# Writing down the order of a GatedDeltaNet + Conformer layer: waits per step in the heads stage, and three engines held to the order in which the kernel is written

## The chip, the cores and the metric

The kernel runs on one core of one Trainium2 chip. The metric is the device time of one execution in microseconds, the median of several runs. Below, PE is TensorE, DVE is VectorE, ACT is ScalarE, POOL is GpSimd, SP is SyncE (it issues the weight loads). Lines L... of this part are those of the kernel before.

## What is computed

One layer on 512 tokens of width 2048, float32, with about 260 MB of weights read once. Cut to what matters here:

```python
h = rmsnorm(x, g_pre)
qkv, z_a, b_raw, a_raw, glu_in, z_b, gate_logits = split(h @ w_in)

# branch A: gated delta rule, 16 heads of 128, chunks of 64 tokens
qkv = silu(causal_depthwise_conv(qkv, w_conv_qkv))      # 4 taps
beta, g_log = sigmoid(b_raw), -exp(a_log) * softplus(a_raw + dt_bias)
A = (k beta) k^T * decay * strict_lower;  T = inverse(I + A)   # per chunk
for each of 8 chunks:                                    # state S, 128x128 per head
    v_new = T(v beta) - T(k beta exp(gc)) S
    o     = (q exp(gc)) S + (q k^T * decay) v_new
    S     = S exp(g_last) + k_end^T v_new
y_a = (rmsnorm(o) * silu(z_a)) @ w_br_a

# branch B: GLU, causal depthwise conv of 31 taps, layernorm, silu, gate
y_b = (silu(layernorm(conv31(glu(glu_in)))) * silu(z_b)) @ w_br_b

mixed = (gate_a * y_a + gate_b * y_b) @ w_out
x = x + rmsnorm(mixed);  x = x + rmsnorm(sigmoid(x @ w_ple_gate) * (p @ w_ple_proj))
```

## The kernel before

The large products run as **tiles** of 48 matmuls 128x512 (`gemm_cm`): each output tile `g` of 128 channels by 512 tokens sums 16 blocks of the inner dimension, and each block takes three matmuls, since every float32 operand is split in a high and a low part (weight high by `rh`, weight high by `rl`, weight low by `rh`; L178, L180, L182). The weights come in pieces of four blocks (12 matmuls). `prep` loads two pieces at a time into `raw` (SP), ACT rounds them to the high part (L125, "CAST w<-raw") and DVE subtracts to get the low part (L126, called the low split below). `next_piece` calls `prep` when fewer than three pieces are ready, so a piece is split two to four pieces ahead of its use; the ring `w` holds four.

All other work is written as Python generators that are spawned with a period and advanced by `tick()` after every large matmul. So a step's place in the program is counted in ticks, one tick being one large matmul. The jobs of the heads stage are, for each of eight groups of two heads: tiles k, q, v of the first head, k, q, v of the second, then `group(g)` is spawned (period HP = 4), then the two z tiles. While the group's generator advances, the tiles z, z of its own and k, q, v, k, q, v of the next group run: 8 x 48 = 384 ticks.

At the end of each k, q or v tile, `conv4` runs the 4-tap convolution out of the tile's PSUM bank: one ACT operation (L404, `cv<-g`), three DVE operations on the same `cv` one after the other (L406), and then a SiLU on ACT (L415 `kc`, L424 `kq`, L431 `vc`).

`group(g)` does, in this order:
- the *prelude*: per head, PE transposes `pk`, `pq`, `pv` into two PSUM buffers of pool `wps`, sums of squares on ACT, scaled copies `ke` and `vh` on DVE, then `pg` (PE) and the masked `W` (DVE);
- the *inversion*: four ACT copies into `Ud` (L575), a DVE transpose `UT`, 31 steps of a DVE product and a DVE reduction (`prod`, `VT`; L591, L592), a transpose `Vd`, four ACT copies into `VP` and DVE transposes `Tc`, then the small PE products `py`, `pz`, `pd`;
- the *scan* (`head_scan`, both heads side by side): eight chunks of PE `psA` (needs the state `S`), DVE `Xz` and ACT `O` from it, PE `psB` (needs `Xz`), ACT `vz` from it, PE `psS` (needs `vz`), DVE `S`. In chunk 0 there is no `psA`, and `Xz` is an ACT copy of `vh` (L455).

After the heads stage come branch A's output tiles interleaved with the gates and the 31-tap convolution (`dwconv`, DVE), then the layer norm and the z tiles of branch B, branch B's output tiles, the output product (Strassen-like, L1016 to L1066) and the last gate.

The order on each engine is not the written one. A scheduler in the library places the instructions by its own model of when each is ready; the written position only ranks them. Its orders are quoted in the section on the change. In the trace each engine's instructions stand in the listed order.

Of the kernel before, what the change touches and what calls it, by code (L numbers as in the profile page):

```python
# [15 lines left out]
P = 128  # L16
T = 512
# [65 lines left out]
def _body(ctx, tc, A, out):  # L83
# [20 lines left out]

    def cc(col, n=P):
        return cst[:, col:col + n]
# [6 lines left out]
    prepped = deque()  # L113

    def prep():
        if not prep_src:
            return
        src = prep_src.popleft()
        raw = rawp.tile([P, 1024], F32, tag="raw", name="raw", bufs=3)
        nc.sync.dma_start(raw, src)  # L120
        for q in range(2):
            rq = raw[:, q * T:(q + 1) * T]
            w = ring.tile([P, 1024], F32R, tag="w", name="w")
            hi, lo = w[:, 0:T], w[:, T:]
            nc.scalar.copy(hi, rq)  # L125
            nc.vector.tensor_tensor(lo, rq, hi.bitcast(F32), ALU.subtract)  # L126
            prepped.append((hi, lo))
# [37 lines left out]
    def gemm_cm(src, rhs, evac):  # L165
# [3 lines left out]
        def job():  # L169
            ps = gps.tile([P, T], F32, tag="g", name="g")  # L170
            for qt in range(4):
                hi, lo = next_piece()
                for kk in range(4):
# [4 lines left out]
                    mm(ps, wh, rh, start=(k == 0), stop=False)  # L178
                    tick()
                    mm(ps, wh, rl, start=False, stop=False)  # L180
                    tick()
                    mm(ps, wl, rh, start=False, stop=(k == NK - 1))  # L182
# [82 lines left out]


# [26 lines left out]
    def beta_decay(ps):  # L293
        sb = hd.tile([32, T], F32, tag="cv", name="ba_cm")
        nc.scalar.copy(sb, ps[0:32, :])
        yield
        pt = wps.tile([P, T], F32, tag="w", name="ba_t")
        for tt in range(NTT):
            nc.tensor.transpose(pt[:, tt * 32:(tt + 1) * 32], sb[:, tt * P:(tt + 1) * P], cst[0:32, C_ID:C_ID + 32])
        yield  # L300
        ptv = pt[:, 0:128].rearrange("p (t x) -> p t x", x=32)
        nc.scalar.activation(beta, ptv[:, :, 0:NH], AF.Sigmoid)
# [5 lines left out]
        def tl(nm):  # L308
# [3 lines left out]
        nc.vector.tensor_tensor(av.rearrange("p (t h) -> p t h", h=NH), ptv[:, :, NH:2 * NH],  # L312
                                vv(V_DT, NH).unsqueeze(1).broadcast_to([P, NTT, NH]), ALU.add)
        na = tl("na")
        nc.vector.scalar_tensor_tensor(na, av, -1.0, av, ALU.mult, ALU.min)
        e = tl("e")
        nc.scalar.activation(e, na, AF.Exp)
        ea = hp1.tile([P, NH], F32, name="ea")
        nc.scalar.activation(ea, vv(V_ALOG, NH), AF.Exp)
        yield  # L320
        den = tl("den")
        nc.vector.tensor_scalar(den, e, 2.0, None, ALU.add)
        rden = tl("rden")
        nc.vector.reciprocal(rden, den)
        z = tl("z")
        nc.vector.tensor_tensor(z, e, rden, ALU.mult)
        z2 = tl("z2")
        nc.vector.tensor_tensor(z2, z, z, ALU.mult)
        s = tl("s")
        nc.vector.tensor_scalar(s, z2, 1.0 / 17.0, 1.0 / 15.0, ALU.mult, ALU.add)  # L330
        for m in range(13, 0, -2):
            nc.vector.tensor_tensor(s, s, z2, ALU.mult)
            nc.vector.tensor_scalar(s, s, 1.0 / m, None, ALU.add)
            yield
        nc.vector.tensor_tensor(s, s, z, ALU.mult)
        r = tl("r")
        nc.vector.tensor_scalar(r, av, 0.0, None, ALU.max)
        sp = tl("sp")
        nc.vector.scalar_tensor_tensor(sp, s, 2.0, r, ALU.mult, ALU.add)
        g = hp1.tile(TH, F32, name="g_log")  # L340
        nc.vector.scalar_tensor_tensor(g, sp.rearrange("p (t h) -> p t h", h=NH), -1.0,
                                       ea.unsqueeze(1).broadcast_to([P, NTT, NH]), ALU.mult, ALU.mult)
# [3 lines left out]
        mm(pc[:, 0:n], cc(C_CUM), gf, start=True, stop=True)  # L346
        mm(pc[:, n:2 * n], cc(C_BLK), gf, start=True, stop=True)
        mm(pc[:, 2 * n:3 * n], cc(C_HALF0), gf, start=True, stop=True)
        mm(pc[:, 3 * n:4 * n], cc(C_HALF1), gf, start=True, stop=True)
# [3 lines left out]
        nc.vector.tensor_copy(gcf, pc[:, 0:n])  # L353
        dl = tl("dl")
        nc.vector.tensor_tensor(dl, pc[:, n:2 * n], gcf, ALU.subtract)
        nc.vector.tensor_scalar(dl, dl, 0.0, None, ALU.min)
        nc.scalar.activation(ek.rearrange("p t h -> p (t h)"), dl, AF.Exp)
        nc.scalar.activation(eS.rearrange("p a t h -> p (a t h)"), pc[:, 2 * n:4 * n], AF.Exp)
        eg = tl("eg")
        nc.scalar.activation(eg, gcf, AF.Exp)  # L360
        nc.vector.tensor_scalar(neg_eg.rearrange("p t h -> p (t h)"), eg, -1.0, None, ALU.mult)
        yield
        pw = wps.tile([P, T], F32, tag="w", name="sw_ps")
        mm(pw[:, 0:n], cc(C_SWAP), eg, start=True, stop=True)
        nc.vector.tensor_copy(eg_sw.rearrange("p t h -> p (t h)"), pw[:, 0:n])
        blk = hp1.tile([P, P], F32R, name="blk")
        nc.vector.tensor_copy(blk, cc(C_BLK))
        gh = hp1.tile(TH, F32R, name="gh")
        nc.vector.tensor_copy(gh, g)
        gl = hp1.tile(TH, F32R, name="gl")  # L370
        nc.vector.tensor_tensor(gl, g, gh.bitcast(F32), ALU.subtract)
        tri = cst[:, C_TRI:C_TRI + 64].unsqueeze(1).unsqueeze(1).broadcast_to([P, 2, NTT, 64])
        for gi in range(NH // 2):
            tg = []
            for eng, src, tag in ((nc.vector, gh, "ke"), (nc.gpsimd, gl, "vh")):
# [7 lines left out]
            mm(pr, blk, tg[0], start=True, stop=False)  # L383
            mm(pr, blk, tg[1], start=False, stop=True)
# [3 lines left out]
            nc.vector.tensor_tensor(ed, pr.rearrange("p (h t i) -> p h t i", h=2, i=64),  # L388
                                    gcv.unsqueeze(3).broadcast_to([P, 2, NTT, 64]), ALU.subtract)
            edf = ed.rearrange("p h t i -> p (h t i)")  # L390
            nc.vector.tensor_scalar(edf, edf, 0.0, None, ALU.min)
            nc.scalar.activation(edf, edf, AF.Exp)
            nc.vector.tensor_tensor(ed.rearrange("p h t i -> p (h t) i"), ed.rearrange("p h t i -> p (h t) i"),
                                    cst[:, C_TRI:C_TRI + 64].unsqueeze(1).broadcast_to([P, 8, 64]), ALU.mult)
# [6 lines left out]
    def conv4(ps, ct):  # L401
        y = hd.tile([P, T], F32, tag="cv", name="cv")
        w0 = V_CONV + ct * 4
        nc.scalar.activation(y, ps, AF.Copy, scale=vv(w0 + 3))  # L404
        for s in range(1, 4):
            nc.vector.scalar_tensor_tensor(y[:, s:], ps[:, 0:T - s], vv(w0 + 3 - s), y[:, s:], ALU.mult, ALU.add)  # L406
# [4 lines left out]
    def evac_k(h):  # L411
        def f(ps):
            y = conv4(ps, 16 + h)
            kc = hd.tile([P, T], F32, tag="kc", name="kc", bufs=2)
            nc.scalar.activation(kc, y, AF.Silu)  # L415
# [5 lines left out]
    def evac_q(h):  # L421
        def f(ps):
            y = conv4(ps, h)
            nc.scalar.activation(hstate[h]["kq"][:, :, 1:3, :], y.rearrange("p (t x i) -> p t x i", x=2, i=64), AF.Silu)  # L424
        return f

    def evac_v(h):
        def f(ps):
            y = conv4(ps, 32 + h)
            vc = hd.tile([P, T], F32, tag="vc", name="vc", bufs=2)  # L430
            nc.scalar.activation(vc, y, AF.Silu)  # L431
# [3 lines left out]
    def evac_z(h):  # L435
        def f(ps):
            z = hd.tile([P, T], F32, tag="za", name="za", bufs=3)
            nc.scalar.activation(z, ps, AF.Silu)
# [3 lines left out]
    def head_scan(g, hh, G):  # L442
# [6 lines left out]
        for c in range(8):  # L449
# [4 lines left out]
            if c == 0:  # L454
                nc.scalar.copy(X[0:64, :], vh[0:64, 0, :])  # L455
            else:
                pa = sps.tile([P, P], F32, tag="s", name="psA")
                mm(pa, kq[:, tt, 2 * par:2 * par + 2, :].rearrange("p x i -> p (x i)"), S, start=True, stop=True)
                yield
                nc.vector.scalar_tensor_tensor(X[a:a + 64, :], pa[a:a + 64, :], neg_eg[a:a + 64, tt, h:h + 1],  # L460
                                               vh[a:a + 64, tt, :], ALU.mult, ALU.add)
                nc.scalar.activation(O[b:b + 64, tt, :], pa[b:b + 64, :], AF.Copy, scale=eg_sw[b:b + 64, tt, h:h + 1])
            pb = sps.tile([P, P], F32, tag="s", name="psB")
            mm(pb, VP[:, x, :, :].rearrange("p x i -> p (x i)"), X, start=True, stop=True)  # L464
            yield
            if c < 7:
                nc.scalar.activation(vt[a:a + 64, :], pb[a:a + 64, :], AF.Copy, scale=c_all[a:a + 64, x:x + 1])
                pS = sps.tile([P, P], F32, tag="s", name="psS")
                mm(pS, ke[:, tt, :], vt, start=True, stop=True)  # L469
                S2 = hd.tile([P, P], F32, tag="S", name="S", bufs=4)  # L470
                if c == 0:
                    nc.vector.tensor_copy(S2, pS)
# [870 lines left out]
```

## Time and profile before

| | |
|---|---|
| median of 3 runs | 2540.99 us (2539.71 to 2543.15) |
| profiled execution, its own time | 2539.74 us |
| its span, first to last instruction | 2537.1 us |
| PE busy | 2495.0 us, 98% of the span, 12202 matmuls |
| DVE busy | 1652.4 us, 65% |
| ACT busy | 1056.8 us, 42% |
| heads stage with the delta rule | about 128 to 1006 us, one group each 111.5 us |

A row of a window gives, for each engine, the busy time in that window and the number of instructions, then the granted TensorE clock as a share of full speed, the DMA share and GB/s. A row of a timeline gives start and duration in us, the engine and its line, the operation, what it writes and reads, how many were merged, and in brackets the idle time of the engine before it and what ended that.

### The profile page before, as it was taken

What the parts mean: (1) busy time and instruction counts of PE and PEld (TensorE: products, weight loads), DVE (VectorE), ACT (ScalarE), POOL (GpSimd) and SP (SyncE); (2) the same over time, 40 slices, a digit from 0 to 9 for tenths busy, and PEclk for the clock granted to TensorE, in tenths of its full rate; (3) what the DMA queues carried; (4) which work ended last, traced back from release to release, by engine and by line L of the source; (5) the groups of instructions that cost most, each with busy time, mean ns of one, the idle gap of its engine ahead of it and who ended that gap; (6) DMA issues with size and microseconds to landing.
All of it is one profiled execution on the core that took longest, in us unless ns stands there. A gap on an engine that the chain in (4) does not pass through costs nothing.

```text
span 2537.1 us, 32634 instructions
## 1 busy us (share of the span) xinstructions
PE 2495.0 (98%) x12202; PEld 2035.7 (80%) x12202; DVE 1652.4 (65%) x3092; ACT 1056.8 (42%) x2083; POOL 140.6 (6%) x151
## 2 busy tenths in 40 slices
PE   8999999999999999999999999999999999999998
PEld 7878787777878777888888888887888888787887
DVE  6765767666676765977786868947433334777644
ACT  6655455455555455322222222225422222544532
POOL 0100000000000000000000000002000000000000
PEclk9999999999999999999999999999999999999999
DMA  6322222222222222333333332442322332677552
GB/s 257 122 87 71 84 72 83 79 75 88 71 84 71 84 67 75 104 105 102 105 97 107 104 107 98 135 135 92 100 99 93 100 99 92 184 214 224 191 174 75
DMA packets 85406, 279.45 MB, mean 110 GB/s; under 512 B 9472, under 2 KB 9728, under 8 KB 85248
## 3 DMA queue, kind: packets, MB, share of 16 engines
q1 hardware_dynamic: 81792, 266.89, 31.5%
q0 software_dynamic: 2304, 8.39, 1.8%
q10 hardware_dynamic: 1152, 2.10, 0.3%
q8 instruction: 95, 1.56, 0.3%
q14 instruction: 63, 0.52, 0.1%
HBM read 262.66 MB, written 14.68 MB: 109 GB/s over the span
## 4 chain that ended last, share of the span: by engine, by line
PE 85%; DVE 9%; ACT 2%; issue 2%; DMA 1%; POOL 0%; SPq 0%; DVEq 0%; POOLq 0%; ACTq 0%
PE g L182 23%; PE g L180 23%; PE g L178 23%; DVE prod L591 2%; PE f L1197 2%; PE f L1198 2%; PE f L1196 2%; DVE w L126 2%; PE psS L469 1%; PE f L1041 1%; PE f L1042 1%; PE f L1040 1%; DVE VT L592 1%; DVE cv L406 1%; PE psB L464 1%
## 5 line engine op out<-in xcount | busy, mean ns | idle before, releaser
L182 PE MATMUL g<-hh,w 128*128 128x512 f32 x2320 | 919.4, 396 | 13.1 <-DVE w L126 13.1
L180 PE MATMUL g<-hl,w 128*128 128x512 f32 x2320 | 915.2, 394 | 0.0
L178 PE MATMUL g<-hh,w 128*128 128x512 f32 x2320 | 914.6, 394 | 0.0
L126 DVE TENSOR_TENSOR w<-raw,w 128x512 fp32r<-128x512 f32 x780 | 549.2, 707 | 483.9 <-ACT w L125 482.8
L125 ACT CAST w<-raw 128x512 fp32r<-128x512 f32 x780 | 478.4, 619 | 893.3 <-PE g L182 789.3
L182 PEld LDWEIGHTS g<-hh,w 128*128 128x128 f32 x2320 | 436.6, 188 | 106.6 <-DVE w L126 21.2
L180 PEld LDWEIGHTS g<-hl,w 128*128 128x128 f32 x2320 | 436.6, 188 | 87.3 <-issue 1.6
L178 PEld LDWEIGHTS g<-hh,w 128*128 128x128 f32 x2320 | 436.8, 188 | 82.9 <-issue 0.2
L673 DVE SCALAR_TENSOR_TENSOR uc<-sg,vec,uc 128x483 f32<-128x483 f32 (+15 forms) x480 | 351.3, 734 | 14.2 <-ACT uc L670 4.3
L406 DVE SCALAR_TENSOR_TENSOR cv<-g,vec,cv 128x511 f32<-128x511 f32 x144 | 107.0, 743 | 32.9 <-ACT cv L404 32.3
L178 PE MATMUL g<-oh,w 128*128 128x512 f32 x256 | 99.6, 389 | 0.0
L180 PE MATMUL g<-ol,w 128*128 128x512 f32 x256 | 99.6, 389 | 0.0
L182 PE MATMUL g<-oh,w 128*128 128x512 f32 x256 | 99.6, 389 | 0.0
L178 PE MATMUL g<-uh,w 128*128 128x512 f32 x256 | 99.6, 389 | 0.0
L180 PE MATMUL g<-ul,w 128*128 128x512 f32 x256 | 99.6, 389 | 0.0
L182 PE MATMUL g<-uh,w 128*128 128x512 f32 x256 | 99.6, 389 | 0.0
L591 DVE TENSOR_TENSOR prod<-UT,VT 128x2 f32<-128x2 f32 (+30 forms) x248 | 87.6, 353 | 7.2
L1041 PE MATMUL f<-wsp,oph 128*128 128x512 f32 x192 | 76.7, 400 | 4.2 <-DVE wsp L1017 4.2
L1197 PE MATMUL f<-w,xh 128*128 128x512 f32 x192 | 75.6, 394 | 2.0 <-DVE w L126 2.0
L1040 PE MATMUL f<-wsp,oph 128*128 128x512 f32 x192 | 75.0, 398 | 1.8 <-ACT wsp L1016 1.8
L1196 PE MATMUL f<-w,xh 128*128 128x512 f32 x192 | 75.8, 396 | 0.0
L1042 PE MATMUL f<-wsp,opl 128*128 128x512 f32 x192 | 75.8, 395 | 0.0
(298 smaller groups left out, 2682.4 us busy)
## 6 DMA issues: line engine op xcount, KB each, us to landing
raw<-in_w_in SPq DMA_DIRECT2D x290, 512.0 KB, 3.3
raw<-in_w_ple_gate SPq DMA_DIRECT2D x40, 512.0 KB, 4.1
raw<-in_w_out SPq DMA_DIRECT2D x35, 512.0 KB, 4.8
raw<-in_w_br_a SPq DMA_DIRECT2D x32, 512.0 KB, 3.3
raw<-in_w_br_b SPq DMA_DIRECT2D x32, 512.0 KB, 3.2
t<-in_w_out POOLq DMA_DIRECT2D x16, 512.0 KB, 7.0
rw<-in_w_out SPq DMA_DIRECT2D x9, 512.0 KB, 4.7
x<-in_x SPq DMA_DIRECT2D x8, 512.0 KB, 9.1
```

Source lines behind the costliest of these rows:

```text
L125: nc.scalar.copy(hi, rq)
L126: nc.vector.tensor_tensor(lo, rq, hi.bitcast(F32), ALU.subtract)
L178: mm(ps, wh, rh, start=(k == 0), stop=False)
L180: mm(ps, wh, rl, start=False, stop=False)
L182: mm(ps, wl, rh, start=False, stop=(k == NK - 1))
L406: nc.vector.scalar_tensor_tensor(y[:, s:], ps[:, 0:T - s], vv(w0 + 3 - s), y[:, s:], ALU.mult, ALU.add)
L591: nc.vector.tensor_tensor(pv_, um, vm, ALU.mult)
L673: nc.vector.scalar_tensor_tensor(y[:, s:], u[:, 0:T - s], vv(w0 + TAPS - 1 - s), y[:, s:], ALU.mult, ALU.add)
L1041: mm(ps, lh, wl[:, c], start=False, stop=False)
L1042: mm(ps, ll, wh[:, c], start=False, stop=kk == 7)
L1196: mm(ps[tt], lh, wh, start=k == 0, stop=False)
L1197: mm(ps[tt], lh, wl, start=False, stop=False)
```

## The change

It has four parts.

1. **Written order.** `pin` ties an instruction behind the one that is written before it on its engine. From after the load of x to the end of branch B, nearly every instruction of PE, DVE and ACT is pinned, the weight splits in `prep` too (`ordered`, while `paced[0]` is set). POOL's instructions and SP's loads stay with the scheduler.
2. **Waits per step.** A generator may now yield a number: the ticks until its next step, in place of its period.
3. **The group is rewritten.** Prelude steps go through both heads before the next kind (pk, pk, pq, pq, pv, pv), `pg` of both heads is one run, `py` and `pz` are one run, the inversion's steps get waits by their size, and the scan gets a wait of two ticks between `vz` and `psS`.
4. In the layer norm, `rstd` and one more `ul` move from pool `s2` to pool `lop`.

The diff, cut to its core (every `nc.vector`, `nc.scalar`, `nc.tensor` call of the stretch that is not shown is wrapped in `pin(...)` in the same way):

```diff
+    pin = tc.keep_in_program_order
...
+    paced = [False]
+    def ordered(ins):
+        if paced[0]:
+            pin(ins)
...
-            nc.scalar.copy(hi, rq)
-            nc.vector.tensor_tensor(lo, rq, hi.bitcast(F32), ALU.subtract)
+            ordered(nc.scalar.copy(hi, rq))
+            ordered(nc.vector.tensor_tensor(lo, rq, hi.bitcast(F32), ALU.subtract))
...
     def spawn(gen, period, key=None):
-        active.append([gen, period, 0, key])
+        active.append([gen, period, period, key])
     def tick():
         for a in list(active):
-            a[2] += 1
-            if a[2] >= a[1]:
-                a[2] = 0
-                if next(a[0], "end") == "end":
+            a[2] -= 1
+            if a[2] <= 0:
+                steps = next(a[0], "end")
+                if steps == "end":
                     active.remove(a)
+                else:
+                    a[2] = steps or a[1]
...
-                    mm(ps, wh, rh, start=(k == 0), stop=False)
+                    pin(mm(ps, wh, rh, start=(k == 0), stop=False))
                     tick()
...
     gemm_cm(None, hT, lambda ps: spawn(beta_decay(ps), 5))
+    paced[0] = True
...
-        nc.scalar.activation(y, ps, AF.Copy, scale=vv(w0 + 3))
+        pin(nc.scalar.activation(y, ps, AF.Copy, scale=vv(w0 + 3)))
         for s in range(1, 4):
-            nc.vector.scalar_tensor_tensor(y[:, s:], ps[:, 0:T - s], vv(w0 + 3 - s), y[:, s:], ALU.mult, ALU.add)
+            pin(nc.vector.scalar_tensor_tensor(y[:, s:], ps[:, 0:T - s], vv(w0 + 3 - s), y[:, s:], ALU.mult, ALU.add))
...   (head_scan)
+                pin(nc.scalar.activation(vt[a:a + 64, :], pb[a:a + 64, :], AF.Copy, scale=c_all[a:a + 64, x:x + 1]))
+                yield 2
                 pS = sps.tile([P, P], F32, tag="s", name="psS")
...   (group)
+        yield
+        pgs = []
+        for hh, h, s4, kq, kc, vc in heads:
             pg = wps.tile([P, NTT, 2, 64], F32, tag="w", name="pg")
...
+            pgs.append(pg)
+        yield 6
...
+        owed, pace = 0.0, 2.6 if g < NH // 2 - 1 else 1.85
         for j in range(30, -1, -1):
...
-            yield
-        for _ in range(3):
-            yield
+            owed += (1.0 + n * ni / 120.0) * pace
+            if owed >= 1:
+                yield int(owed)
+                owed -= int(owed)
+        yield
...   (after the copies into VP and Tc)
-        for _ in range(6):
-            yield
+        yield 10
...   (py, then pz without a yield between, then)
+        yield 6
...   (Y and VP from them, then)
+        yield 8
...   (pd, then)
+        yield 6
...   (layer norm)
-        rstd = s2.tile([P, T], F32, tag="s2", name="rstd")
+        rstd = low(0, "rstd", F32)
...
+    paced[0] = False
```

How this moves instructions, at the three places that the prediction speaks of. All three are in the third group; lines of the changed kernel are ten to thirty higher than those of before.

**ACT, end of a v tile, where the scan begins.** `cv<-g` opens the convolution, `vc<-cv` is its SiLU, `CAST w<-raw` the weight splits, `vz<-psB` the scan's chunk 0. Before:

```order
L632 COPY VP<-pd 32x8x32 x2
L404 ACTIVATE cv<-g,vec 128x512
L125 CAST w<-raw 128x512
L467 ACTIVATE vz_536<-psB,c_all 64x128
L477 COPY O<-psB 64x128
L467 ACTIVATE vz_538<-psB,c_all 64x128
L477 COPY O<-psB 64x128
L431 ACTIVATE vc<-cv 128x512
```

Now:

```order
L651 COPY VP<-pd 32x8x32 x2
L415 ACTIVATE cv<-g,vec 128x512
L442 ACTIVATE vc<-cv 128x512
L133 CAST w<-raw 128x512 x2
L466 COPY Xz_532<-vh 64x128
L466 COPY Xz_534<-vh 64x128
L478 ACTIVATE vz_536<-psB,c_all 64x128
L478 ACTIVATE vz_538<-psB,c_all 64x128
```

The SiLU has moved ahead of two casts, the two copies into `Xz` (they were far up, in the prelude, before) and the `vz` of chunk 0. On PE, `psB` of chunk 0 stands two matmuls into the tile that follows, and one before.

**DVE, end of the next k tile, in the scan at chunks 3 and 4.** `cv<-g,vec,cv` are the three convolution operations, `w<-raw,w` the low splits. Before:

```order
L406 SCALAR_TENSOR_TENSOR cv<-g,vec,cv 128x511
L126 TENSOR_TENSOR w<-raw,w 128x512
L406 SCALAR_TENSOR_TENSOR cv<-g,vec,cv 128x510
L474 SCALAR_TENSOR_TENSOR S<-S,eS,psS 128x128
L406 SCALAR_TENSOR_TENSOR cv<-g,vec,cv 128x509
L479 TENSOR_TENSOR O<-O,psB 64x128
L474 SCALAR_TENSOR_TENSOR S<-S,eS,psS 128x128
```

Now:

```order
L417 SCALAR_TENSOR_TENSOR cv<-g,vec,cv 128x511
L417 SCALAR_TENSOR_TENSOR cv<-g,vec,cv 128x510
L417 SCALAR_TENSOR_TENSOR cv<-g,vec,cv 128x509
L134 TENSOR_TENSOR w<-raw,w 128x512 x2
L486 SCALAR_TENSOR_TENSOR S<-S,eS,psS 128x128
L491 TENSOR_TENSOR O<-O,psB 64x128
```

Both `S` now stand behind the whole convolution and both low splits. At the end of the q tile after it, the two `Xz` of chunk 7 stand behind the same row of five.

**DVE, end of a q tile, at the end of the inversion.** Before, from the last but one step on:

```order
L406 SCALAR_TENSOR_TENSOR cv<-g,vec,cv 128x509
L592 TENSOR_REDUCE VT<-prod 128x8
L126 TENSOR_TENSOR w<-raw,w 128x512
L591 TENSOR_TENSOR prod<-UT,VT 128x256
L592 TENSOR_REDUCE VT<-prod 128x8
L597 STREAM_TRANSPOSE Vd<-VT 128x256
```

Now:

```order
L611 TENSOR_TENSOR prod<-UT,VT 128x256
L612 TENSOR_REDUCE VT<-prod 128x8
L417 SCALAR_TENSOR_TENSOR cv<-g,vec,cv 128x511
L417 SCALAR_TENSOR_TENSOR cv<-g,vec,cv 128x510
L417 SCALAR_TENSOR_TENSOR cv<-g,vec,cv 128x509
L134 TENSOR_TENSOR w<-raw,w 128x512 x2
L619 STREAM_TRANSPOSE Vd<-VT 128x256
```

`Vd` has the q tile's convolution and two low splits ahead of it, where before it followed the last step at once. PE's small runs keep their places in ticks: `py` stands 26 matmuls after that tile's end now, and 24 before.

More of the change, by code (lines that the diff above doesn't have):

```diff
@@ L294, in beta_decay @@
         sb = hd.tile([32, T], F32, tag="cv", name="ba_cm")
-        nc.scalar.copy(sb, ps[0:32, :])
+        pin(nc.scalar.copy(sb, ps[0:32, :]))
         yield
@@ L637, in group @@
         while scans:
+            wait = None
             for s in list(scans):
-                if next(s, "end") == "end":
+                got = next(s, "end")
+                if got == "end":
                     scans.remove(s)
-            yield
+                else:
+                    wait = got
+            yield wait
     for g in range(NH // 2):
@@ L762, in layer_norm @@
         pm = lps.tile([P, T], F32, tag="l", name="mean_ps")
-        mm(pm, ones, acc[0], start=True, stop=True)
+        pin(mm(pm, ones, acc[0], start=True, stop=True))
         mean = low(0, "mean", F32)
-        nc.vector.tensor_scalar(mean, pm, 1.0 / D, None, ALU.mult)
+        pin(nc.vector.tensor_scalar(mean, pm, 1.0 / D, None, ALU.mult))
         acc2 = low(0, "acc2", F32)
@@ L789, in layer_norm @@
         prs = lps.tile([P, T], F32, tag="l", name="rstd_ps")
-        mm(prs, ones, dg, start=True, stop=True)
-        rstd = s2.tile([P, T], F32, tag="s2", name="rstd")
-        nc.scalar.copy(rstd, prs)
+        pin(mm(prs, ones, dg, start=True, stop=True))
+        rstd = low(0, "rstd", F32)
+        pin(nc.scalar.copy(rstd, prs))
         yield
@@ L800, in layer_norm @@
                 yield
-            nc.vector.tensor_tensor(u, u, zb[i], ALU.mult)
+            pin(nc.vector.tensor_tensor(u, u, zb[i], ALU.mult))
             uh = low(0, "uh")
-            nc.scalar.copy(uh, u)
-            ul = low(LOP if i < 32 - LOP else 0, "ul")
-            nc.vector.tensor_tensor(ul, u, uh.bitcast(F32), ALU.subtract)
+            pin(nc.scalar.copy(uh, u))
+            ul = low(LOP if i < 33 - LOP else 0, "ul")
+            pin(nc.vector.tensor_tensor(ul, u, uh.bitcast(F32), ALU.subtract))
             uT[i] = (uh, ul)
@@ L811, in f @@
             z = low(0, "zb", F32)
[L812 removed]
+            pin(nc.scalar.activation(z, ps, AF.Silu))
             zb[i] = z
```

259 lines of the change are left out of this document (127 added, 132 removed).

## The prediction

> **What bounds the kernel now.** I read the page first, then the windows by stage, then the waits of TensorE, and then the timeline of one group.
>
> ```profile
> span 2537.1 us, 32634 instructions
> PE 2495.0 (98%) x12202; PEld 2035.7 (80%) x12202; DVE 1652.4 (65%) x3092; ACT 1056.8 (42%) x2083; POOL 140.6 (6%) x151
> ...
> 300.00:400.00 100.00, 98.66 (x506) 79.85 (x505) 68.92 (x181) 51.69 (x127) 8.19 (x9) 1.00 0.22 73
> 1100.00:1200.00 100.00, 100.00 (x443) 82.81 (x442) 79.41 (x116) 26.95 (x44) 2.59 (x2) 1.00 0.30 100
> ...
> 300.00:400.00 100.00, 90.28 (x354) 63.81 (x355) 11.14 (x15) 4.19 (x7) 1.00 0.22 73
> ```
>
> TensorE bounds it. Outside the heads stage (window 1100 to 1200) it never waits and starts a large matmul every 100 / 443 = 0.226 us; that is one tick. In the heads stage only 354 of those 443 starts fit in 100 us (the last row counts the instructions on `g` alone): the rest goes to small runs and waits. What the change can gain or lose is there. Three things show what a small run and a wait cost:
>
> ```profile
> PE g L182 <- DVE w L126: 13.1, 10, 2.8
> PEld psS L469 <- ACT vz L467: 20.3, 64, 0.5
> PE po L498 <- DVE O L493: 1.2, 1, 1.2
> ...
> L469 PE MATMUL psS<-vz,ke 128*128 128x128 f32 x224 | 42.7, 302 | 0.7
> L458 PE MATMUL psA<-S,kq 128*128 128x128 f32 x224 | 38.6, 274 | 0.0
> ```
>
> TensorE waits 13.1 us for low splits that come late, and its weight loads wait 20.3 us for `vz`, of which only 224 x (302 - 274) ns = 6.3 us appears in the matmuls themselves. Those are the waits the change can remove, with 1.2 us at the scan's last transposes.
>
> **What the tile's end looks like.** This is the end of one k tile inside a scan; the rows are of PE, ACT and DVE.
>
> ```profile
> 427.77 0.40 PE L182 MATMUL g<-hh,w 128*128 128x512 f32 x1
> 428.01 0.61 PE L464 MATMUL psB<-Xz,VP 128*128 128x128 f32 x4
> 428.69 0.39 PE L180 MATMUL g<-hl,w 128*128 128x512 f32 x1
> ...
> 428.21 0.69 ACT L404 ACTIVATE cv<-g,vec 128x512 f32<-128x512 f32 x1 [0.15 <-PE g L182]
> 428.80 0.61 ACT L125 CAST w<-raw 128x512 fp32r<-128x512 f32 x1
> 429.31 0.62 ACT L467 ACTIVATE vz<-psB,c_all 64x128 f32<-64x128 f32 x2
> 432.85 0.62 ACT L415 ACTIVATE kc<-cv 128x512 f32<-128x512 f32 x1
> ...
> 428.93 0.75 DVE L406 SCALAR_TENSOR_TENSOR cv<-g,vec,cv 128x511 f32<-128x511 f32 x1 [1.27 <-ACT cv L404]
> 429.60 0.68 DVE L126 TENSOR_TENSOR w<-raw,w 128x512 fp32r<-128x512 f32 x1
> 430.20 0.74 DVE L406 SCALAR_TENSOR_TENSOR cv<-g,vec,cv 128x510 f32<-128x510 f32 x1
> 430.86 0.34 DVE L474 SCALAR_TENSOR_TENSOR S<-S,eS,psS 128x128 f32<-128x128 f32 x1
> 431.11 0.74 DVE L406 SCALAR_TENSOR_TENSOR cv<-g,vec,cv 128x509 f32<-128x509 f32 x1
> ...
> 395.13 0.64 ACT L415 ACTIVATE kc<-cv 128x512 f32<-128x512 f32 x1 [8.44 <-DVE cv L406]
> 395.67 0.61 ACT L125 CAST w<-raw 128x512 fp32r<-128x512 f32 x1
> ```
>
> The scheduler let ACT do the cast and `vz` ahead of the SiLU, and let DVE slip a low split and `S` between the convolution's operations, so TensorE runs on. The last pair shows what happens otherwise: ACT sat 8.44 us at a SiLU that waited for the convolution, with a cast queued behind it. The first three rows also price a small run: from 427.77 to 428.69 lie two large matmuls (0.45) and one run of four, so 0.47 us.
>
> **The written order at a tile's end.** Let s be the start of the tile's last matmul (427.77 above). `cv` starts at s + 0.44 and ends at s + 1.13; the convolution's operations start at s + 1.16 and follow at 0.67 and 0.66, the last taking 0.74, so they end at s + 3.23. Only then the SiLU: s + 3.26 to 3.88. An ACT row follows its neighbour about 0.1 before that one's end (428.80, 429.31), so the two casts end at 4.39 and 4.90; an `Xz` copy (0.30) ends at 5.10. On DVE, the two low splits start at 4.42 and 5.02 (0.60 apart, as 429.60 and 430.20), and the next operation at 5.62, ending at 5.97.
>
> - Chunk 0 (v tile): `psB` stands two matmuls into the next tile, due at s + 3 x 0.226 = 0.68, and needs the `Xz` copy at 5.10. Wait 4.4 us.
> - Chunk 4 (k tile): `psA` is due after two matmuls, a `psS` run and four more: 0.68 + 0.47 + 0.90 = 2.05. It needs both `S`, at 5.97 and about 0.5 later. Wait 4.2 us.
> - Chunk 7 (q tile): `psB` is due after the `psA` run and four matmuls: 0.23 + 0.47 + 0.90 = 1.60, and needs `Xz` at 5.97. Wait 4.4 us.
>
> TensorE is pinned too, so no large matmul can fill these. They come to 13.0 us a group, in seven groups (behind the eighth run z, gate and GLU tiles, without a convolution): 91 us. The chain could be shorter by 0.5 each if sequencing gaps overlap (80), longer if the raw load is late (98).
>
> **The prelude and the inversion.** These rows carry it:
>
> ```profile
> 346.33 0.28 ACT L530 ACTIVATE junk<-pk 128x128 f32<-128x128 f32 x1
> 347.70 0.20 ACT L530 ACTIVATION_READ_ACCUMULATOR junk<-pk 128x1 f32 x1
> ...
> 359.68 8.16 ACT L575 COPY Ud<-W 32x1024 f32<-32x1024 f32 x4 [1.41 <-DVE W L561]
> 367.86 0.60 ACT L438 ACTIVATE za<-g 128x512 f32<-128x512 f32 x1
> ...
> 367.87 1.25 DVE L581 STREAM_TRANSPOSE UT<-Ud 128x1024 f32<-128x1024 f32 x1 [7.33 <-ACT Ud L575]
> 370.35 0.15 DVE L591 TENSOR_TENSOR prod<-UT,VT 128x2 f32<-128x2 f32 x1
> 397.03 0.69 DVE L597 STREAM_TRANSPOSE Vd<-VT 128x256 f32<-128x256 f32 x1
> 397.75 2.81 ACT L603 COPY VP<-Vd 32x256 f32<-32x256 f32 x4 [1.47 <-DVE Vd L597]
> 401.23 0.69 PE L611 MATMUL py<-Tc,W 32*32 32x32 f32 x32
> ```
>
> Prelude: the group starts right after a v tile, so its squares (four on `pk` take 347.90 - 346.33 = 1.57) queue behind SiLU and casts: s + 4.80 to 6.4. `pq` needs that buffer at tick 16, s + 0.23 + 3.62 + two runs = 4.8: a wait of 1.6, and 0.7 more at the second `pv` by the same count. 2.3 us a group.
>
> `Ud`: ACT is blocked 8.16 us, and now the z tile's `za` and both casts stand behind it. They need `W` and not the tick, so they start about 1 us before tick 46 (my estimate), and tick 72 falls 1 + 26 x 0.226 + 0.3 = 7.2 us after their start. Its piece has its high part at 8.16 + 0.52 + 0.61 = 9.3 and its low part at 10.0, which is needed 0.45 later than the high part. Wait 2.4 us a group.
>
> Inversion: DVE comes out of `Ud` late (two low splits, then `UT`, and 1.28 from `UT` to the first product: 11.8 us after the copies' start). From first product to `Vd` before are 26.7 us; less nine low splits and three convolution operations that lie between (7.4), the 31 steps take 19.3. Now twelve low splits (7.2), two convolutions (4.0) and twice a wait for SiLU and cast (1.2) come with them: `Vd` at 11.8 + 19.3 + 7.2 + 4.0 + 2.4 = 44.7, and `py` follows `Vd` by 401.23 - 397.03 = 4.2, so 48.9. TensorE would be there at 7.2 + 2.4 + 146 x 0.226 = 42.6. Wait 6.3 us a group, most at `py`, some at late low splits before it. The waits by size thus don't help: DVE is behind, not ahead. If DVE were not behind, `py` would still wait about 3.8 (chain of the q tile's end, 5.62 + 4.2, against tick 26, 6.1); a lag of 2 us more gives 8. In the eighth group the faster pace gives 7 us.
>
> So 11.0 us in each of eight groups: 88 us, between half of it and 100. `beta_decay` meets one tile end in the same way: 4 us.
>
> **The clock.** After long waits the profile shows TensorE at half clock:
>
> ```profile
> 949.40:952.30 2.90, 0.08 (x2) 0.05 (x1) 2.77 (x6) 0.00 (x0) 0.00 (x0) 1.00 0.00 0
> 953.00:956.40 3.40, 3.40 (x9) 2.65 (x9) 2.27 (x6) 3.30 (x6) 0.00 (x0) 0.51 0.44 154
> 2346.30:2348.40 2.10, 0.14 (x2) 0.07 (x1) 2.10 (x5) 0.62 (x2) 0.00 (x0) 1.00 0.00 0
> 2349.10:2352.50 3.40, 3.40 (x9) 2.63 (x8) 2.34 (x6) 0.75 (x2) 0.70 (x1) 0.50 0.83 259
> 391.90:393.20 1.30, 0.06 (x2) 0.02 (x1) 1.30 (x3) 0.00 (x0) 0.00 (x0) 1.00 0.00 0
> 393.20:396.60 3.40, 3.40 (x15) 2.67 (x16) 3.37 (x7) 1.14 (x2) 0.77 (x1) 1.00 0.41 154
> ```
>
> Idle stretches of about 2 and 2.9 us are followed by 3.4 us at clock 0.5, with 9 matmuls where 15 went through after a wait of 1.3. That costs 6 x 0.226 = 1.4 us each time. The four long waits (three in the scan, `py`) happen 4 x 7 + 1 = 29 times: 41 us; none if the clock were left alone, twice that if two windows follow each wait.
>
> [...]
>
> **What it gains.** The two ticks between `vz` and `psS` take away its wait: between 6.3 and 20.3 us. I take 11, nearer the lower end, since a load waits while matmuls before it still run. Late low splits go in their old form: 12 of the 13.1. Fewer runs: pairs never split (212 psA, psB and psS runs become 176) and three runs fewer a group, 60 at 0.1 to 0.2 us that a run costs beyond its matmuls: 8. The eighth group's shorter waits end it before its jobs do: 1. Together 32, between 25 and 45. Past the heads stage I cost the pins at nothing: TensorE has no small run that waits there, and splits are two pieces, 5.4 us, ahead; if a DVE queue used that up, each 43 us cycle of four tiles would add up to 1 us. `rstd` and `ul` change a buffer only.
>
> **Sum.** 91 + 88 + 4 + 41 - 32 = 192 us on the profiled 2539.74, and 1.25 more, by which the median of the runs stands above it: 2733.
>
> **Rivals.**
> - *The removed waits decide: faster.* If ACT and DVE reached `Xz` and `S` in time, only the gain is left: 2541 - 32 = 2509. It decides if the chain to `Xz` is under 0.7 to 2.1 us after a tile's end; the rows above make it 5.1 to 6. Chance 3%.
> - *Only the scan waits.* If prelude, `Ud` and inversion are hidden (a lag of DVE that I overestimate): 91 + 21 x 1.4 - 32 = 88, so 2629. Against it: `Ud` blocked ACT to the very edge already before (`za` at 367.86). Up to 2645: 8%.
> - *Half of those waits, or no clock loss*: 2645 to 2690. 16%.
> - *Two slow windows a wait, or late splits throughout*: 2795 and more. 6%.
> - *No effect* would need the pins to leave the order as it was; the lists show that they don't. 1%.
>
> **How the numbers follow.** The main case, 2690 to 2795, has 66%, and the predicted time is its sum. With the 16% next to it the range is 2645 to 2795. 0.2% (5 us) is what a measurement of this kernel can tell from no change: faster 3%, same 1%, slower 96%.
>
> **What would show it.** The waits of TensorE after: `psB` for `Xz` from ACT, `psA` for `S`, `psB` for `Xz` from DVE, each with singles over 4 us and seven or more times; `py` for the `Tc` transposes; `psS` for `vz` gone. A group's period of about 111.5 + 24 + 6 - 4 = 137 us, a mean clock near 0.98, stages past the heads unchanged. It is wrong if the SiLU holds up nothing that TensorE needs, or if the long waits stay under 2 us.

## The result, and the profile after

| | before | after |
|---|---|---|
| median of 5 runs | 2540.99 us | 2816.86 us (2815.55 to 2819.6) |
| ratio, 95% interval | | 1.1086 (1.1073 to 1.1099) |
| profiled execution | 2539.74 us | 2816.43 us |

The kernel became slower by 276 us; 192 were forecast. The measurement lies outside the range that I gave, above its end of 2795. Lines are those of the changed kernel from here on. The first lines of its page, with the row of TensorE's granted clock in tenths, and the mean clock of the core:

```profile
span 2814.7 us, 32533 instructions
...
PE 2581.6 (92%) x12202; PEld 2106.5 (75%) x12202; DVE 1664.9 (59%) x3092; ACT 1042.2 (37%) x2081; POOL 130.2 (5%) x151
...
PEclk9898989898989898999999999999999999999999
```

```profile
core 0: 2814.7 us, clock 0.957
```

TensorE does the same 12202 matmuls, and two things have changed. The time in which it is not busy went from 2537.1 - 2495.0 = 42.1 to 2814.7 - 2581.6 = 233.1 us: 191 more. And its busy time went up by 86.6 us although no work was added: that is the clock, which stands at 8 tenths in every other one of the first 16 slices, in the heads stage. The windows that were shown of before, now:

```profile
300.00:400.00 100.00, 84.78 (x468) 67.89 (x468) 55.73 (x136) 41.27 (x90) 4.19 (x6) 0.90 0.21 66
1100.00:1200.00 100.00, 85.35 (x423) 69.46 (x423) 52.68 (x147) 43.78 (x109) 5.91 (x7) 0.93 0.16 53
...
300.00:400.00 100.00, 74.15 (x278) 53.65 (x278) 8.96 (x12) 3.95 (x6) 0.90 0.21 66
```

278 large matmuls in that 100 us where there were 354, at a mean clock of 0.90. The second window now still lies in the heads stage, which lasts to about 1265 us. TensorE's waits (in all, times, longest, in us):

```profile
PE g L188 <- ACT w L133: 45.2, 27, 3.8
PE psB L475 <- DVE Xz L471: 35.8, 9, 4.7
PE psB L475 <- ACT Xz L466: 34.3, 8, 4.6
PE psA L469 <- DVE S L486: 30.2, 9, 4.1
PE py L632 <- DVE Tc L626: 27.5, 16, 3.0
PE pq L556 <- DVE ke L544: 20.2, 8, 2.5
...
PE gc_ps L357 <- DVE g_log L352: 5.5, 1, 5.5
PE g L192 <- DVE w L134: 5.2, 5, 1.5
...
PE psS L481 <- ACT vz L478: 0.2, 1, 0.2
```

The three waits of the scan are rows 2 to 4. This is the one of chunk 4, at the end of a k tile; rows of TensorE, VectorE and ScalarE from the timeline:

```profile
684.58 0.39 PE L192 MATMUL g<-hh,w 128*128 128x512 f32 x1
689.11 1.24 PE L469 MATMUL psA<-S,kq 128*128 128x128 f32 x4 [4.15 <-DVE S L486]
...
683.90 2.32 DVE L417 SCALAR_TENSOR_TENSOR cv<-g,vec,cv 128x511 f32<-128x511 f32 x3 [2.66 <-ACT cv L415]
687.51 1.29 DVE L134 TENSOR_TENSOR w<-raw,w 128x512 fp32r<-128x512 f32 x2 [1.28 <-ACT w L133]
688.72 0.34 DVE L486 SCALAR_TENSOR_TENSOR S<-S,eS,psS 128x128 f32<-128x128 f32 x1
...
686.34 0.63 ACT L426 ACTIVATE kc<-cv 128x512 f32<-128x512 f32 x1 [2.47 <-DVE cv L417]
686.87 1.12 ACT L133 CAST w<-raw 128x512 fp32r<-128x512 f32 x2
```

VectorE ends the convolution at 686.22, only then ScalarE runs the SiLU, then the casts; VectorE idles 1.28 us for them, does two low splits, and only then `S`. TensorE has meanwhile waited 4.15 us; 4.2 were forecast.

In this trace the clock changes only at the borders of windows of 3.413 us, on one grid from end to end (each border lies on it to within 0.005 us). Here are the four around the same wait one group later (at 828.34), and four around the `pq` wait (at 872.3); TensorE's busy time and count, then the clock:

```profile
826.94:830.35 3.41, 1.40 (x9) 1.00 0.00 0
830.35:833.76 3.41, 1.28 (x5) 0.50 0.13 36
833.76:837.18 3.42, 3.42 (x11) 0.50 0.30 117
837.18:840.59 3.41, 3.41 (x20) 1.00 0.00 0
...
871.31:874.72 3.41, 0.99 (x5) 1.00 0.14 19
874.72:878.14 3.42, 3.32 (x10) 0.50 0.34 134
878.14:881.55 3.41, 3.41 (x21) 1.00 0.11 19
881.55:884.96 3.41, 3.41 (x35) 1.00 0.39 139
```

One wait of 4.1 us has two windows at half clock behind its start, and a wait of 2.5 us, which the forecast let pass, has one. All in all the clock is at half for 245.5 us (46 stretches), 20.2 before (4 stretches); the last stretch of each, 6.6 and 10.0 us, lies behind the last matmul. While TensorE works there are thus 70 windows at half clock, and 3 before.

### The profile page after: what moved, and what is told of

The parts are those of the page before. It is cut to its first block, busy times and chain, and to the rows that moved or that the text cites. A ratio compares the mean times of both kernels' runs of the same rounds, so it can differ in the third digit from the quotient of the medians.

```text
span 2814.7 us, 32533 instructions
## 1 busy us (share of the span) xinstructions
PE 2581.6 (92%) x12202; PEld 2106.5 (75%) x12202; DVE 1664.9 (59%) x3092; ACT 1042.2 (37%) x2081; POOL 130.2 (5%) x151
## 4 chain that ended last, share of the span: by engine, by line
PE 71%; DVE 15%; ACT 7%; issue 4%; DMA 2%; SPq 0%; ACTq 0%; POOL 0%; DVEq 0%; POOLq 0%
PE g L192 18%; PE g L190 18%; PE g L188 18%; DVE cv L417 4%; DVE prod L611 3%; DVE w L134 3%; DVE VT L612 2%; ACT Ud L594 2%; ACT w L133 2%; PE f L1221 2%; PE f L1222 2%; PE f L1220 2%; PE psB L475 2%; DMA raw<-in_w_out 1%; PE f L1065 1%
## 5 line engine op out<-in xcount | busy, mean ns | idle before, releaser
L188 PE MATMUL g<-hh,w 128*128 128x512 f32 x2320 | 934.8, 403 | 45.2 <-ACT w L133 45.2
L192 PE MATMUL g<-hh,w 128*128 128x512 f32 x2320 | 939.1, 405 | 5.2 <-DVE w L134 5.2
L190 PE MATMUL g<-hl,w 128*128 128x512 f32 x2320 | 938.4, 404 | 0.0
L134 DVE TENSOR_TENSOR w<-raw,w 128x512 fp32r<-128x512 f32 x780 | 522.9, 698 | 526.1 <-ACT w L133 523.7
L188 PEld LDWEIGHTS g<-hh,w 128*128 128x128 f32 x2320 | 450.4, 194 | 145.0 <-ACT w L133 56.9
L192 PEld LDWEIGHTS g<-hh,w 128*128 128x128 f32 x2320 | 450.7, 194 | 105.2 <-DVE w L134 17.1
L696 DVE SCALAR_TENSOR_TENSOR uc<-sg,vec,uc 128x511 f32<-128x511 f32 (+16 forms) x480 | 351.9, 738 | 11.2
L475 PE MATMUL psB<-Xz,VP 128*128 128x128 f32 x256 | 49.5, 324 | 70.3 <-DVE Xz L471 35.8
L475 PEld LDWEIGHTS psB<-Xz,VP 128*128 128x128 f32 x256 | 44.0, 224 | 84.9 <-DVE Xz L471 42.9
L188 PE MATMUL g<-oh,w 128*128 128x512 f32 x256 | 99.6, 389 | 0.0
L188 PE MATMUL g<-uh,w 128*128 128x512 f32 x256 | 99.6, 389 | 0.0
L486 DVE SCALAR_TENSOR_TENSOR S<-S,eS,psS 128x128 f32<-128x128 f32 x96 | 32.9, 343 | 95.3 <-PE psS L481 94.6
L473 ACT ACTIVATE O<-psA,eg_sw 64x128 f32<-64x128 f32 x112 | 36.0, 362 | 140.2 <-DVE Xz L471 139.7
L415 ACT ACTIVATE cv<-g,vec 128x512 f32<-128x512 f32 x48 | 33.0, 688 | 140.4 <-PE g L192 140.3
```

Of the source, the lines that this page charges most:

```text
L134: ordered(nc.vector.tensor_tensor(lo, rq, hi.bitcast(F32), ALU.subtract))
L188: pin(mm(ps, wh, rh, start=(k == 0), stop=False))
L190: pin(mm(ps, wh, rl, start=False, stop=False))
L192: pin(mm(ps, wl, rh, start=False, stop=(k == NK - 1)))
L475: pin(mm(pb, VP[:, x, :, :].rearrange("p x i -> p (x i)"), X, start=True, stop=True))
L696: pin(nc.vector.scalar_tensor_tensor(y[:, s:], u[:, 0:T - s], vv(w0 + TAPS - 1 - s), y[:, s:], ALU.mult, ALU.add))
```

## The experiments

My theory: the blocks of work at a tile's end (convolution, SiLU, casts, low splits) stand in front of what the scan needs, and TensorE's waits then also cost clock. The rivals: the rewritten group costs; TensorE's own fixed order costs; the clock costs little. All times in this table are medians against a median of before of 2539 to 2541 us; "idle" is the time between the end of a matmul and the start of the next (so without the 15 us ahead of the first and behind the last), "half" the busy time of TensorE at half clock, both added up from the trace of one execution.

| kernel | us | ratio (interval) | idle | half |
|---|---|---|---|---|
| before | 2541 | | 26.6 | 10.2 |
| after | 2817 | 1.1086 (1.1073 to 1.1099) | 217.8 | 192.9 |
| e1, nothing pinned | 2537 | 0.9987 (0.9978 to 0.9996) | 35.6 | 11.3 |
| e2, pins, old group | 2782 | 1.0957 (1.0941 to 1.0973) | 179.0 | 184.0 |
| e3, TensorE pinned | 2565 | 1.0107 (1.009 to 1.0125) | 51.8 | 18.7 |
| e4, ACT and DVE pinned | 2639 | 1.0394 (1.0379 to 1.041) | 80.1 | 76.9 |
| e5, convolution spread | 2659 | 1.0469 (1.0453 to 1.0485) | 112.4 | 72.2 |
| e5b, SiLU later | 2704 | 1.0644 (1.0627 to 1.0662) | 137.0 | 142.4 |
| e7, waits filled | 2757 | 1.0855 (1.0839 to 1.0871) | 86.9 | 54.3 |
| e10, no scan wait | 2835 | 1.1161 (1.1146 to 1.1177) | 232.2 | 197.2 |
| e12, three chains spread | 2604 | 1.0252 (1.0238 to 1.0266) | 73.1 | 54.3 |
| e15, e5 without pins | 2537 | 0.9988 (0.9979 to 0.9997) | 37.3 | 19.1 |

**Which part of the change (e1 to e4).**

```diff
 e1:  def pin(ins): return ins
 e2:  group() as before, every PE, ACT and DVE call pinned; no "yield 2" in head_scan
 e3:  pin only mm and nc.tensor.transpose
 e4:  pin only nc.scalar and nc.vector (weight splits too)
```

> The changed kernel with no instruction pinned: the scheduler orders all engines again; the rewritten group and its waits stay. Theory (the written order makes TensorE wait, the rewrite itself costs nothing): 2500 to 2545 us, no single wait over 4 us in the scan. Rival (the rewrite and its waits make the group longer): 2650 us or more.

> The changed kernel with the group's generator of before (one step per period, no merged runs, no wait between vz and psS), all pinned. Theory (the order alone does it): 2800 to 2870 us, with the three scan waits of 4 to 5 us a group. Rival (the rewrite is what costs): 2541 to 2650 us.

> The changed kernel with TensorE's instructions alone pinned; VectorE, ScalarE and the weight splits are left to the scheduler. Theory (what VectorE and ScalarE have in front of Xz and S is what costs): 2510 to 2580 us. Rival (TensorE's own fixed order costs, since its runs stand too early): 2700 us or more.

> The changed kernel with VectorE, ScalarE and the weight splits pinned and TensorE left to the scheduler. Theory (TensorE waits only because nothing else may go ahead of the small run): the small runs move behind more large matmuls, the long waits go for the most part: 2545 to 2680 us. Rival (the late chain makes the group longer than its tiles whatever TensorE's order): 2750 us or more.

Without pins the rewritten group runs as before did (2537), and the order alone, on the old group, makes 2782. So the order is the cause. e1, e3 and e4 lie in the ranges of their theories. Against e1, TensorE's order alone costs 28 us, the order of ScalarE and VectorE alone 103, both together 280: most of the loss needs the two at once, late producers and a TensorE that may put nothing else in front of the consumer. In e4 the scan's long waits are gone; most of what is left are waits of large matmuls for the high part of their weights, 50 us in all and 4.0 the longest. In e2 the time came out 18 under the range that I gave, and the scan waits under theirs: the rewrite, which I credited with a gain, costs 35 us under pins. Two rows of e2's waits:

```profile
PE psS L480 <- ACT vz L478: 54.3, 17, 3.8
PE g L188 <- ACT w L133: 54.1, 21, 3.6
```

In the old group the scan meets two tile ends with `psS`, four ticks into the next tile, and a third with `po`, 16 ticks in; in a steady group these wait 3.7, 3.8 and 2.3 us, 9.8 together. In the new one three runs stand 2 to 6 ticks in and wait 4.6, 4.1 and 4.7, 13.4 together. The chain at a tile's end is the same; what differs is how long after it the run is due. Over the whole run that is 29 of the 39 us of idle time between the two. The inversion differs less: in e2 `py` doesn't wait, but the large matmuls around it wait 1.3 and 3.6 us for their weights, 4.9 against 5.7 us a group.

**The scan's wait of two ticks (e10).**

```diff
-                yield 2
                 pS = sps.tile([P, P], F32, tag="s", name="psS")
```

> The changed kernel, all pinned, without the wait of two ticks between vz and psS (the period of 4 runs on through vz and psS as one step). A chunk is then 12 ticks instead of 14, eight chunks 96 instead of 112, two tiles instead of two and a third. Theory (the longer scan meets a third tile end, and so a third long wait): one wait of 4.5 us and its half-clock window go in seven groups, psS waits for vz come back at 5 to 10 us in all: 2775 to 2795 us. Rival (the two ticks only take away the wait for vz): 2817 to 2837 us.

My theory for e10 fell, and the rival's range holds the time. The shorter scan doesn't meet fewer tile ends, it meets them elsewhere:

```profile
PE psB L475 <- DVE Xz L471: 55.7, 21, 5.5
...
PE psB L475 <- ACT Xz L466: 34.3, 8, 4.6
...
PE po L509 <- DVE O L504: 24.7, 8, 3.5
```

`psB` now stands two ticks after the second tile end, not four after the third, and waits 5.5 us; the third end is met by `po`, which waits 3.5; two waits of 1.2 are new. Together 16.1 us a group against 13.4. That the places of the runs also make most of the difference between e2 and the changed kernel is read from the waits; it was not tried by itself.

**The chain at the tile's end (e5, e5b, e12).**

```diff
 def conv4(...):
     pin(nc.scalar.activation(y, ps, AF.Copy, ...))
-    for s in range(1, 4): pin(nc.vector.scalar_tensor_tensor(y[:, s:], ...))
-    return y                                  # the SiLU followed at once
+    def later():                              # e5: one step every 4 ticks
+        for s in range(1, 4):
+            pin(nc.vector.scalar_tensor_tensor(y[:, s:], ...)); yield
+        silu(y)
+    spawn(later(), 4)                         # e5b: only silu(y), after 14 ticks
```

> The changed kernel, all pinned, with the convolution's three VectorE operations and the SiLU written 4, 8, 12 and 16 ticks into the next tile instead of at its start. Theory (this chain in front of Xz and S makes the three scan waits): ScalarE has cv and two casts ahead of Xz (copy at s + 2.7, due at 0.68: wait 2.0), VectorE two low splits (S at s + 3.5, due at 2.05: 1.5; Xz at 3.5, due at 1.60: 1.9), so 13.4 us a group become about 5.4, and four of nine half-clock windows a group go: 7 x (8.0 + 4 x 1.4) = 95 us less, and up to 30 less in prelude and inversion: 2680 to 2735 us. Rival (the splits or the scan's own chain hold it up): 2790 us or more.

> The changed kernel, all pinned, with the SiLU alone written 14 ticks later; the three convolution operations stay at the tile's end. Theory: casts and low splits no longer stand behind the SiLU, so the waits become about 2.0 (chunk 0), 2.8 (chunk 4) and 3.2 (chunk 7), 8.0 in place of 13.4, and one window of half clock a group less: 7 x (5.4 + 1.4) = 48 us less, 2755 to 2785 us. Rival (the SiLU holds up nothing, the convolution's operations alone do): 2805 us or more.

Moving one ScalarE instruction per tile (e5b) takes away 113 us, moving the convolution as well 158. The sizes were right for the scan (in a steady group 1.5, 2.8 and 3.3 us in e5b, where 2.0, 2.8 and 3.2 were expected; 1.5, 1.2 and 1.6 in e5, where 2.0, 1.5 and 1.9 were), but both times came out below the range. In e5b `pq` no longer waits either (0.4 in place of 2.5, and I had not counted it), and the wait of 1.5 us brings no half clock.

In e12 nothing is unpinned; two further blocks are written in pieces:

```diff
 prep():   the pair of weight pieces is split by a generator, 3 and 9 ticks on
 group():  after each of the first three copies into Ud
+            yield 8
```

> All pinned, the convolution spread as in e5_conv_spread (2659 us), and two more chains spread: of a pair of weight pieces the first is split 3 and the second 9 ticks after the place where both stood, and the four copies into Ud stand 8 ticks apart, so that casts come between them. Theory (the written order costs only where a block of work stands in front of what TensorE needs next): the scan's three waits fall from 1.2 to 2.0 us to under 1.2, the 2.3 us wait of the prelude's Ud goes, with the half-clock windows that they bring: 2590 to 2630 us. Rival (fixed order costs in itself, wherever the blocks stand): 2645 us or more.

2604, within the range: 213 of the 276 us are gone with every engine still held to the written order. The four largest sums of TensorE's waits in it:

```profile
PE psB L489 <- DVE Xz L485: 14.7, 15, 1.1
PE po L524 <- DVE ke L558: 10.3, 7, 1.5
PE pk L553 <- DVE oa L532: 9.2, 7, 1.3
PE py L648 <- DVE Tc L642: 8.1, 9, 1.7
```

From the first scan to the end of the heads stage no wait is longer than 1.7 us; `beta_decay`, ahead of it, still has one of 2.3. So most of the loss came from the blocks. 65 us over before remain; by the table they are again idle time (46) and clock (21). How much of them a fixed order costs wherever the blocks stand was not tried.

> The kernel of e5_conv_spread with no instruction pinned. Theory (the scheduler already moves the convolution out of the way, so its written place hardly matters): 2525 to 2540 us, as without pins (2537). Rival (the written place matters for the scheduler's ranking too): below 2520 or above 2550 us.

Left to the scheduler, the convolution's written place makes no difference (e15, 2537). e1 and e15 are the two versions that come out ahead of both kernels, by 0.13% and 0.12% of before, which is less than the 0.2% that I would call faster.

**The clock by itself (e7, e9).** In e7 TensorE does needless matmuls while it would wait:

```diff
+    def fill(n):
+        for _ in range(n):
+            pin(mm(cur[0], zw, hT[0][0], start=False, stop=False))   # zw is zero, cur[0] the running tile
...  fill(20) before psB of chunks 0 and 7, fill(18) before psA of chunk 4 (seven groups),
...  fill(11) before pq of head 0, fill(10) before py (eight groups)
```

> The changed kernel, all pinned, with 79 extra large matmuls a group (zero weights, added to the tile that runs) in front of the five waits: 20, 18, 20 at the scan's three, 11 at pq, 10 at py, each as long as the wait there. The waits' length stays, TensorE is busy in them. Theory (the clock costs about 1.4 us for each half-clock window, and 7 of 9 windows a group come from these waits): 49 to 58 windows fewer, 2735 to 2765 us. Rival 1 (half clock costs next to nothing, the waits are the whole loss): 2812 to 2830 us. Rival 2 (1.7 us a window): 2718 to 2735 us.

```profile
L417 PE MATMUL g<-hh,zw 128*128 128x512 f32 x574 | 139.9, 395 | 0.0
```

574 more large matmuls, 574 x 0.2265 = 130 us of work, and the kernel is 60 us faster (2757, in the range of the theory and outside those of both rivals). Idle time fell by 217.8 - 86.9 = 131 us: the work took the place of the waits one for one. What was saved is the clock: 66.6 us at half in place of 245.5.

e9 leaves out the layer. It only runs large matmuls, with 117 waits of set length between them; its figures are of one execution.

> Not the layer: large matmuls on one operand, interrupted 117 times by a chain of VectorE operations that TensorE waits for, 13 lengths from about 0.5 to 5 us, nine times each, 14 to 18 us apart. It prices idle time alone. Theory (the clock is set window by window on a fixed grid of 3.413 us: a window that is idle for over about 1.9 us is followed by one at half clock): none up to 1.7 us, mostly one window from 2.0 to 3.4, one or two from 3.8 to 5, by where the wait lies on the grid. Rival (each wait beyond a length is followed by one window wherever it lies): always one from 2 us on.

| wait, us | half-clock windows after it, of nine waits |
|---|---|
| 0.55 to 1.53 (four lengths) | never |
| 1.86, 2.19 | none five times, one four times |
| 2.52 | none three times, one six times |
| 2.84 | none three times, one five times, two once |
| 3.17 | none twice, one four times, two three times |
| 3.50 | none once, one three times, two five times |
| 3.83 to 4.48 (three lengths) | one 14 times, two 13 times |

The theory held, with one difference: at 2.19 us, where it said mostly one window, five waits of nine brought none. The rival falls, since waits of the same length had different effects. Two waits of 2.19 us show the grid at work, and two of 4.15 why some cost two windows; in groups of windows of e9 in a row:

```profile
858.23:861.65 3.42, 2.67 (x12) 1.00 0.00 0
861.65:865.06 3.41, 1.98 (x9) 1.00 0.00 0
865.06:868.47 3.41, 3.41 (x17) 1.00 0.00 0
...
916.26:919.67 3.41, 1.23 (x6) 1.00 0.00 0
919.67:923.09 3.42, 3.42 (x10) 0.50 0.00 0
923.09:926.50 3.41, 3.41 (x16) 1.00 0.02 5
...
2056.31:2059.72 3.41, 0.59 (x3) 1.00 0.00 0
2059.72:2063.14 3.42, 2.08 (x5) 0.50 0.02 5
2063.14:2066.55 3.41, 3.41 (x9) 0.50 0.00 0
...
2172.36:2175.78 3.42, 1.97 (x9) 1.00 0.00 0
2175.78:2179.19 3.41, 0.71 (x3) 1.00 0.00 0
2179.19:2182.60 3.41, 3.41 (x10) 0.50 0.03 5
```

The first wait lies across a border, no window is idle for more than 1.43 us, and the clock stays full; the second lies within one window, idle for 2.18 us, and the next is at half clock. Of the long ones, the third makes the window in which it begins idle for 2.82 us, and the next is at half clock; its rest, 1.34 us, lies in that one, and the one behind is at half clock as well. The fourth begins late in its window, which is idle for 1.44 us, and the next is still at full clock; only that one, idle for 2.70 us, is followed by one at half. By starts, an undisturbed full window holds 15.0 matmuls and a half one 8.0 (mean of 52): a half window costs 7 x 0.227 = 1.6 us.

## Why the prediction was right or wrong

The table's last two columns account for nearly the whole. By the counts of e9, a microsecond of busy time at half clock loses 7/15 = 0.47 us. From before to after: idle 217.8 - 26.6 = 191; clock (192.9 - 10.2) x 7/15 = 85; together 276 of the 277.6 us between the two spans. The same sum gives 67 for e12 (span 67.7 longer), 211 for e7 with its 130 us of filler (218.5), 234 for e2 (243.3) and 85 for e4 (98.9): what it leaves open is up to 14 us.

- **The scan's waits: right.** 4.4, 4.2 and 4.4 forecast, 4.6, 4.1 and 4.7 in a steady group, and by the chain that the prediction worked out. 94 us in seven groups for the 91 of the sum, and 6 more in the eighth, where I expected none.
- **Prelude, `Ud`, inversion: right in sum.** 2.5, 2.25 and 5.7 us a group against 2.3, 2.4 and 6.3. In the prelude the sum was luck: I gave 1.6 to `pq` and 0.7 to the second `pv`; `pq` alone waits 2.5 and `pv` not at all. In the inversion `py` waits 3.35, and the rest, 1.65 and 0.7, are large matmuls ahead of it that wait for the cast of their weights (`g` L188 <- ACT), not for low splits as I wrote.
- **`beta_decay`: mis-sized.** I gave it 4 us, one meeting with a tile's end. TensorE waits five times there (5.5, 1.9, 2.6, 3.8, 2.1): 15.9. The last four are for casts. Three of those stand behind a SiLU ahead of which ScalarE runs a table load of 1.28 us (at 89.63, 106.37 and 127.92 us in the trace), one behind an exponential that itself waited 7.7 us for VectorE.
- **The clock: the step that failed.** 29 windows at 1.4 us, 41 in the sum; it was 85. The count was too small: 67 windows more than before. A steady group has eight where I counted four: one each for chunk 0, chunk 7 and the `pq` wait of 2.5 us, two for chunk 4, three around `py`; six more lie in `beta_decay`. My own rows had full clock after a wait of 1.3 us and half clock after one of 2.1, and yet I counted only the four long waits and let those between 1.6 and 4 us pass. The price of 1.4 was not what failed: a window at half clock without idle time costs 1.6 (the rows' 9 and 15 include matmuls cut by the window's ends), but in the layer TensorE is idle in part of many such windows, so 85 / 67 = 1.3 each. The rival of two slow windows a wait had 6%; it was nearest to what happened.
- **The gains: the other step that failed.** 32 forecast. The late splits of before went, but that is within the idle sum. The 11 us for `psS` came: its matmuls take 144 ns each before and 95 now (in runs at full clock, from the large matmul ahead to the one behind, less one tick), 11 us over 224. The 8 us for fewer runs did not: by the same count `psA` goes from 88 to 97 ns and `psB` from 92 to 106, and already before, a pair of them took 0.14 to 0.18 us where a run of four took 0.37, so that splitting such a run cost nothing. Beyond idle and clock the account leaves 1 us of the wrong sign, where I had 19; so about 12 us are lost that neither shows, up to 6 of them in `psA` and `psB`; the rest stays open, and is no more than what the account leaves open in other runs.
- Past the heads stage, where I put nothing, TensorE's waits over 0.3 us add up to 16.7 us after and 10.9 before; in the layer norm they are 2.7 in place of 1.6. So TensorE does wait there, though not in the one window that the prediction showed.

The miss is thus 21 us of idle time, 44 of clock and 20 of gains: about 85 in all. It shows in the signs that the prediction named, too: the waits are the ones foretold, but a group takes 143.4 us where 137 were expected, and the mean clock is 0.957, not 0.98. In the whole run half clock cost 192.9 x 7/15 = 90 us by the counts of e9; in the other 53 of the 245.5 us at half clock TensorE was not busy.

## What to carry to other kernels

An order held on all engines costs as much as the blocks of work that stand in front of something urgent (276 us here, 65 with three chains in pieces): before fixing it, look at what stands between the last producer and the next consumer at each place where several chains start at once, and write long chains in pieces between the steps that the bounding engine needs. Where TensorE must wait, ask for each wait how long it makes a clock window idle (in e9 1.96 of its 3.41 us were always followed by half clock, 1.85 never), and add up short waits that lie close together (in e12 two of 1.5 and 1.3 us in one window brought a half one). And count a small run's place from the chain that blocks it, not in runs per tile: in a steady group `psB` of chunk 7, four ticks into its tile, waits 4.7 us, and `psA` of chunk 4, six ticks in, 4.1.

## What the runs showed of the hardware

- In the changed kernel and in e9 the granted clock changed only at the borders of windows of 3.413 us. In e9, from the second window on, every window at full clock that was idle for 1.96 us or more was followed by one at half clock, none idle for 1.85 or less was; in between it went both ways. In the changed kernel the border is less sharp: six windows idle for 1.69 to 1.80 us were followed by one at half clock, seven idle for 1.88 to 1.91 were not.
- In a window of e9 already at half clock, idle time of 0.61 us or more kept the next one at half, and 0.52 or less did not. By an estimate from these limits, both are about the same share of the work that a full window holds: (3.41 - 1.9) / 3.41 = 0.44 of a full window, and (3.41 - 0.57) / 3.41 x 0.5 = 0.42.
- e7's 574 matmuls with zero weights kept the clock up: they took 179 of the 245.5 us at half clock away.
- In six groups of the changed kernel a window with `py` and `pz`, idle for 0.12 us or less, was followed by one at half clock:

```profile
785.98:789.39 3.41, 1.65 (x7) 1.00 0.00 0
789.39:792.80 3.41, 0.28 (x2) 0.50 0.46 154
792.80:796.22 3.42, 3.32 (x63) 0.50 0.13 18
796.22:799.63 3.41, 3.41 (x9) 0.50 0.40 141
```

The first window is one of the six of the border above (idle 1.76 us). The third was busy for 3.32 us, with 63 matmuls: 30 of `py` (32x32), 32 of `pz` (64x64) and one large one. What brought the half clock behind it was not tried by itself.
